# A chunked RWKV-7 and GLA layer on one core: Beta and k turned by VectorE and a DRAM bounce, the read-out without additions, and a new order

## The chip, the core and the metric

The kernel runs on one core of a Trainium2 chip. A core has five engines with instruction streams of their own, which meet only at semaphores: TensorE (PE; its weight loads are listed as PEld), VectorE (DVE), ScalarE (ACT), GpSimd (POOL) and SyncE (SP), which here issues every DMA. The metric is the device time of one execution in microseconds; lower is better.

## The reference

One inference step of one layer for a prompt of 1024 tokens and 8 single new tokens, all in float32. Two branches read the same projection of x and are merged by gates. The part around the change is the RWKV-7 branch: 16 heads of 64, taken in 8 pairs of heads.

```python
p = einsum('btd,dn->btn', x, w_in)                  # 1024 -> 9360 columns
...
prev = concatenate([shift0[:, None], p_rwkv[:, :-1]], axis=1)
pr = p_rwkv + (prev - p_rwkv) * rwkv_mu             # the token before, mixed in
r, kb, vb, g_b, w_lr, aa_lr = split(pr)
w = exp(-0.606531 * sigmoid(rwkv_w0 + tanh(w_lr) @ rwkv_w2))
a = sigmoid(rwkv_a0 + aa_lr @ rwkv_a2)
kk = normalised(kb * rwkv_k_k)
kb = kb * (1.0 + (a - 1.0) * rwkv_k_a)
# for each token and head, S is 64x64:
S = S * w + (S @ -kk) (kk * a)^T + v k^T
y = S @ r
...
m = sigmoid(gate_a) * (o_gla @ w_up_gla) + sigmoid(gate_b) * (o_rwkv @ w_up_rwkv)
y_out = layernorm(2**0.25 * x + m @ w_out)
```

The outputs are y for both groups, the last states of both branches and the last projected rows.

## The kernel before

**Tiles and stages.** The prompt is worked in two passes of 512 tokens; the 8 single tokens go with the first. Channels lie on the partitions, tokens along the free dimension. The projections are blocks of 128 output channels. Each float32 operand is split into two parts of a faster type (`xh`/`xl` and `wpart`), and a block is 8 x 3 matmuls for each of its token tiles: 256 and 264 tokens in the first pass, 512 in the second. The first pass loads the weights (`wraw`), splits them and stores the split parts to DRAM (`w`); the second reads them back. After the blocks of w_in of both passes come the two up-projections, then the output projection with the layer norm.

**A pair of heads.** `pair` runs `front`, `back`, `turn`, `chain` and `norm`. `front` makes the decays and the operands of 8 chunks of 64 tokens: `AZ` (from kk and r), `BK` (Beta, which is kk times a, and k, both divided by the decay), the masked products `GG` of the two, and the inverse of a triangular matrix for each chunk. The inverse is a loop of 31 steps on GpSimd with a multiplication and an addition in each; its operand goes to DRAM (`LD`) and comes back in another layout, and so does its result (`XD`). `back` completes the inverse on TensorE. `turn` transposes `BK` chunk by chunk on TensorE, four to a PSUM bank, with a copy back into `BK`, and then v. `chain` walks through the 8 chunks, three matmuls each (PSUM tag `pch`), and ends with the read-out: for each chunk and head three products in 64\*64 tiles, spread over the four quadrants of the array and over two PSUM banks `pY_`, one for each half of the contraction. So each output is the sum of two banks: three copies and three additions on VectorE (`places`). `norm` normalises and stores the result.

**The token shift.** `shift` evacuates a projection block: ScalarE scales it by 1 - mu (`omu`), VectorE adds mu times the same block one token earlier. In the second pass the first token needs the first pass's last one, which is kept in `tail`: one VectorE instruction on a single column, 33 times.

**The order.** All of it is written as generators of operations (`Stream`), and a planner (`Order.run`) chooses, operation after operation, which goes next, from estimated prices (`price`), the estimated time at which each engine and operand is free, and priorities (`PRIO`, `FOR_PE`, `AGE`, `ASIDE`, `URGENT`, `STAND`, `SCARCE`, `PER_ROW`). The program is the order that it finds, and each engine runs its part in that order; SP too, so a DMA that waits holds those behind it. `E` is an engine of either kind: the planner takes VectorE or GpSimd. `C` takes ScalarE or VectorE. `GATES` says how many gate blocks follow each pair's blocks, `EARLY_GATES`, `SPARE_ROWS` and `RAWS` how far gate rows and inputs are loaded ahead. `row` is a pool of 40 buffers of 128x520.

The profile attributes nearly everything to line 234, where the helper records every operation; tile names tell the groups apart. `big<-cons,wide` are the transposes of `BK` (`cons` holds the identity, `wide` is `BK`), `big<-cons,row` others, those of v among them; `big<-az,gg` and `big<-gg,wide` in 64\*64 tiles are the read-out; `row<-row,big` of 64x256 and 128x256 are its additions.

## Time and profile before

| what | us |
|---|---|
| median of three runs (1447.72 to 1448.53) | 1448.14 |
| the profiled execution, its own time | 1447.86 |
| its span, first instruction to last | 1446.1 |
| TensorE busy | 1432.1 |
| VectorE busy | 1071.7 |
| ScalarE busy | 824.3 |
| GpSimd busy | 379.6 |
| time between the profiled time and its span | 1.8 |

How to read it: busy time is the union of an engine's instructions within the span. Matmuls are pipelined: the duration of one is its latency, and neighbours overlap, so what a matmul occupies is read from the distance of starts in the timeline. A form such as "64\*64 64x64" is rows by columns of the array that the stationary operand takes, and then the size of the output. A float32 product appears as two records, a float32 transpose as one.

### The profile page before, as it was taken

The numbers are of one execution on the slowest core, as the hardware profiler recorded it, in microseconds if no ns is written. First come the engines' busy times: TensorE is split into PE (matmuls) and PEld (weight loads), VectorE is DVE, ScalarE is ACT, GpSimd is POOL, SyncE is SP. The second block draws the span as 40 slices with busy tenths as digits, with TensorE's granted clock in tenths as the row PEclk, the third lists the DMA queues.
The fourth block names the chain that finished last, engine by engine and source line by source line (L and its number), as shares of the span: only waits on it lengthen the run. The fifth ranks groups of instructions, "written<-read, shape, count | busy, mean of one in ns | idle before, by whom it ended". The sixth has DMA issues, their size and how long they took to land.

```text
span 1446.1 us, 31531 instructions
## 1 busy us (share of the span) xinstructions
PE 1432.1 (99%) x11280; PEld 1262.7 (87%) x11280; DVE 1071.7 (74%) x2213; ACT 824.3 (57%) x2035; POOL 379.6 (26%) x1138
## 2 busy tenths in 40 slices
PE   9999999999999999999999999999999999999997
PEld 8999999999999998888788888888788897897786
DVE  7687668976688767783877795978597967676585
ACT  6565658675777575754665655564556656654210
POOL 1061416142324250605060615140523050000000
PEclk9999999999999999999999999999999999999999
DMA  9786877758876688657665655646676677898842
GB/s 327 259 285 217 251 274 252 246 173 309 265 275 224 231 258 291 193 157 218 195 185 153 206 172 169 208 134 204 199 228 190 194 231 246 269 300 273 271 128 86
DMA packets 213625, 323.42 MB, mean 224 GB/s; under 512 B 91955, under 2 KB 107452, under 8 KB 213468
## 3 DMA queue, kind: packets, MB, share of 16 engines
q1 hardware_dynamic: 213468, 321.39, 69.5%
q8 instruction: 90, 1.47, 0.4%
q14 instruction: 67, 0.55, 0.1%
HBM read 201.65 MB, written 118.61 MB: 221 GB/s over the span
## 4 chain that ended last, share of the span: by engine, by line
PE 92%; DVE 4%; DMA 2%; ACT 1%; issue 1%; SPq 0%; DVEq 0%; ACTq 0%
PE proj L234 59%; PE big L234 27%; PE pch L234 6%; DVE row L234 1%; DVE wpart L234 1%; DMA wraw<-w_in 1%; DMA wraw<-w_up_gla 0%; DVE xl L234 0%; DMA row<-xT 0%; DMA row<-w_out 0%; ACT wpart L234 0%; DVE wide L234 0%; DMA row<-o_rwkv 0%; DVE XT L234 0%; ACT row L234 0%
## 5 line engine op out<-in xcount | busy, mean ns | idle before, releaser
L234 PE MATMUL proj<-xh,wpart 128*128 128x512 f32 (+3 forms) x3728 | 910.1, 328 | 0.0
L234 PEld LDWEIGHTS proj<-xh,wpart 128*128 128x128 f32 x3728 | 620.2, 188 | 51.5 <-issue 5.0
L234 PE MATMUL proj<-xl,wpart 128*128 128x512 f32 (+3 forms) x1864 | 610.0, 327 | 0.0
L234 PEld LDWEIGHTS proj<-xl,wpart 128*128 128x128 f32 x1864 | 351.3, 188 | 25.3 <-issue 2.8
L234 POOL TENSOR_TENSOR Xt<-X,wide 128x60 f32<-128x60 f32 (+24 forms) x496 | 166.1, 335 | 522.0 <-DMA wide<-LD 204.4
L234 DVE TENSOR_TENSOR row<-row 128x512 f32<-128x512 f32 (+6 forms) x348 | 180.0, 529 | 15.7 <-ACT row L234 10.5
L234 DVE TENSOR_TENSOR wpart<-wraw,wpart 128x512 fp32r<-128x512 f32 x210 | 145.8, 700 | 59.5 <-ACT wpart L234 57.0
L234 ACT CAST wpart<-wraw 128x512 fp32r<-128x512 f32 x210 | 129.7, 621 | 97.1 <-PE proj L234 50.5
L234 POOL TENSOR_TENSOR X<-X,Xt 128x60 f32<-128x60 f32 (+24 forms) x496 | 168.5, 340 | 38.7
L234 ACT ACTIVATE row<-row 128x520 f32<-128x520 f32 (+4 forms) x229 | 138.2, 610 | 14.9 <-DMA row<-sg 6.7
L234 PE MATMUL big<-xh,wpart 128*128 128x256 f32 (+3 forms) x544 | 125.7, 319 | 0.6 <-ACT xh L234 0.4
L234 DVE TENSOR_TENSOR wide<-pch,gg 64x65 f32<-64x65 f32 x224 | 49.6, 222 | 65.7 <-PE pch L234 63.6
L234 PEld LDWEIGHTS big<-xh,wpart 128*128 128x128 f32 x544 | 90.0, 188 | 8.0 <-ACT xh L234 0.6
L234 ACT COPY rh<-pch 128x130 f32<-128x130 f32 x118 | 31.7, 268 | 105.8 <-PE pch L234 104.9
L234 PE MATMUL big<-xl,wpart 128*128 128x256 f32 (+3 forms) x272 | 86.9, 320 | 0.4 <-DVE xl L234 0.3
L234 ACT COPY row<-big 128x128 f32<-128x128 f32 (+8 forms) x176 | 55.6, 341 | 54.1 <-PE big L234 50.2
L234 POOL TENSOR_TENSOR row<-row 128x256 f32<-128x256 f32 (+3 forms) x21 | 24.5, 1180 | 213.0 <-DVE row L234 122.0
L234 DVE SCALAR_TENSOR_TENSOR row<-proj,pv,row 128x255 f32<-128x255 f32 (+1 forms) x95 | 54.6, 574 | 34.5 <-ACT row L234 28.1
L234 ACT COPY wide<-pch 64x65 f32<-64x65 f32 x232 | 48.2, 208 | 52.3 <-PE pch L234 49.2
L234 ACT ACTIVATE row<-proj,omu 128x256 f32<-128x256 f32 (+1 forms) x95 | 52.0, 547 | 39.1 <-PE proj L234 37.4
L416 ACT ACT_TABLE_LOAD x56 | 71.8, 1283 | 1.0
L234 PE MATMUL big<-row 128*64 128x64 f32 (+4 forms) x648 | 64.8, 272 | 0.0
(220 smaller groups left out, 2117.5 us busy)
## 6 DMA issues: line engine op xcount, KB each, us to landing
w<-wpart SPq DMA_DIRECT2D x146, 512.0 KB
wpart<-w SPq DMA_DIRECT2D x146, 512.0 KB
wraw<-w_in SPq DMA_DIRECT2D x146, 256.0 KB
wide<-LD SPq DMA_DIRECT2D x64, 128.0 KB
wraw<-w_up_gla SPq DMA_DIRECT2D x32, 256.0 KB
row<-w_out SPq DMA_DIRECT2D x32, 256.0 KB
wraw<-w_up_rwkv SPq DMA_DIRECT2D x32, 256.0 KB
sg<-row SPq DMA_DIRECT2D x16, 260.0 KB
```

Source lines behind the costliest of these rows:

```text
L234: ways.append((eng, lambda call=call: call(out, *args, **kw), price(eng, name, out, args, ins)))
L416: self.nc.scalar.preload_act_table_set(self.table)
```

## The change

- **Beta and k.** The 8 transposes on TensorE and 2 copies in `turn` are gone. In `front`, VectorE turns `BK` in blocks of 32x32, two instructions of 128x512, each written whole to a DRAM tile `BT`. Four DMAs read `BT` back into `BK` with the blocks in their places, 32 partitions each, in runs of 32 floats. They are issued behind steps 4, 9, 14 and 19 of GpSimd's loop.
- **The read-out.** The products with the state (`s0`) stay in 64\*64 tiles, one for each chunk and head. The two products with `uf` become one over all 128 rows, in a 128\*64 tile. Both accumulate in the same bank and half, so each output is whole, and four copies of 64x256 take the place of three copies and three additions.
- **The rate factor**, te = ka * a + (1 - ka), goes from VectorE or GpSimd to ScalarE (16 times).
- **The edge column.** In the second pass ScalarE evacuates the first column by itself, with mu times the old last token as its bias. `tail` is multiplied by mu once, when all 33 blocks of the first pass have been evacuated (`edged`); the second pass's evacuations wait for that count.
- **The order.** The planner's priorities and the constants of the gate blocks, inputs and spare rows are set anew.

```diff
-RAWS = 5
+RAWS = 6
...
-SPARE_ROWS = 11
-EARLY_GATES = 13
-GATES = [[2, 1, 3, 0, 3, 2, 2, 3], [2, 1, 2, 2, 2, 3, 1, 3]]
+SPARE_ROWS = 10
+EARLY_GATES = 12
+GATES = [[1, 1, 3, 0, 3, 2, 2, 4], [1, 1, 3, 2, 1, 3, 1, 4]]
...
-AGE = 1.593
+AGE = 2.117
...
-ASIDE = 2.254
+ASIDE = 1.655
...
-FOR_PE = {"pair": 0.502, "turn": 1.611, "chain": 0.743, "norm": 0.181, "lora": 1.468, "rank": 2.14,
-          "head": 0.532, "gate": 2.004, "state": 3.339, "out": 0.822}
-STAND, SCARCE, PER_ROW = 0.037, 0.036, 0.038
-URGENT = 1.733
+FOR_PE = {"pair": 0.438, "turn": 2.001, "chain": 1.193, "norm": 0.187, "lora": 3.947, "rank": 2.131,
+          "head": 0.435, "gate": 1.614, "state": 3.803, "out": 1.518}
+STAND, SCARCE, PER_ROW = 0.037, 0.036, 0.042
+URGENT = 2.628
...
 # shift
-            yield A.activation(dst[:, t0:t0 + m], q[:, lead:lead + m], AF.Copy, scale=omu)
+            if i:
+                yield lambda: self.edged == NRC
+                yield A.activation(dst[:, :1], q[:, :1], AF.Identity, scale=omu, bias=self.tail[:, 0, j:j + 1])
+                yield A.activation(dst[:, 1:m], q[:, 1:m], AF.Copy, scale=omu)
+            else:
+                yield A.activation(dst[:, t0:t0 + m], q[:, lead:lead + m], AF.Copy, scale=omu)
...
             if i:
-                yield V.scalar_tensor_tensor(dst[:, :1], self.tail[:, 0, j:j + 1], mu, dst[:, :1], ALU.mult, ALU.add)
                 yield A.copy(self.tail[:, 0, j:j + 1], q[:, n - 1:n])
-            elif tt == last and smp is not None:
+            elif tt == last:
+                self.edged += 1
+                if self.edged == NRC:
+                    o = PV["mu"][0]
+                    yield V.tensor_mul(self.tail[:, 0], self.tail[:, 0], self.pv[:, o:o + NRC])
+            if i == 0 and tt == last and smp is not None:
                 yield V.scalar_tensor_tensor(smp, self.shT[:, j], mu, dst[:, HT:c.n], ALU.mult, ALU.add)
...
 # front
-        yield E.tensor_scalar(te, td, self.pvec("ka", p), self.oka[:, p:p + 1], ALU.mult, ALU.add)
+        yield A.activation(te, td, AF.Identity, scale=self.pvec("ka", p), bias=self.oka[:, p:p + 1])
...
+        BT = self.dr.tile([P, NCH * P], F32, name=f"BT{c.i}{p}")
+        for f in range(2):
+            y = yield from self.row(HT)
+            yield V.transpose(y, BK_[:, f * HT:(f + 1) * HT])
+            yield self.S.dma_start(BT[:, f * HT:(f + 1) * HT], y)
+            self.free(y)
+        b5 = BT.rearrange("(a i) (x b j) -> b i x a j", a=4, b=4, j=32)
         tm = yield from self.get("Xt")
         for j in range(31):
...
+            if j % 5 == 4 and j < 20:
+                b = j // 5
+                yield self.S.dma_start(BK[32 * b:32 * b + 32].rearrange("i x (a j) -> i x a j", a=4), b5[b])
...
 # turn
-        for x in range(0, NCH, 4):
-            pt = yield from self.bank("big", [P, 4, P])
-            for n in range(4):
-                yield self.tr(pt[:, n], d.BK[:, x + n])
-            yield self.C.copy(d.BK[:, x:x + 4], pt)
-            self.free(pt)
...
 # chain
-        todo = [[[] for _ in HS] for _ in HS]
-        for x in range(NCH):
-            for h, hs in enumerate(HS):
-                ks, out = HS[1 - h], (h + 2 * x // NCH) % 2
-                todo[h][out] += [(x, d.s0[hs, x, vs[h]], AZ[hs, x, 1]), (x, uf[hs, x, vs[h]], GG[hs, x, 1, h])]
-                todo[1 - h][out] += [(x, uf[ks, x, vs[h]], GG[ks, x, 1, h])]
-        yield together([self.P.matmul(pY[r][HS[o], x], w, m, start=(n == 0), stop=(n == len(todo[0][0]) - 1),
-                                      skip_group_check=True)
-                        for n in range(len(todo[0][0])) for r in range(2) for o in range(2) for x, w, m in [todo[r][o][n]]])
-        n = NCH // 2 * C
-        places = [(d.y[:, :n], slice(0, P), slice(0, n))] + [(d.y[hs, n:], ks, slice(n, 2 * n)) for hs, ks in (HS, HS[::-1])]
-        for y, ps, ns in places:
-            yield self.C.copy(y, pY_[0][ps, ns])
-        for y, ps, ns in places:
-            yield V.tensor_add(y, y, pY_[1][ps, ns])
+        H = NCH // 2
+        half = [[(x, HS[(h + x // H) % 2]) for x in range(NCH)] for h in range(2)]
+        order = [(h, x + H * f) for x in range(H) for f in range(2) for h in range(2)]
+        yield together([self.P.matmul(pY[h][half[h][x][1], x], d.s0[HS[h], x, vs[h]], AZ[HS[h], x, 1], start=(x % H == 0),
+                                      stop=False, skip_group_check=True) for h, x in order] +
+                       [self.P.matmul(pY[h][half[h][x][1], x], uf[:, x, vs[h]], GG[:, x, 1, h], start=False, stop=True,
+                                      skip_group_check=True) for h, x in order])
+        y3 = d.y.rearrange("p (c t) -> p c t", c=NCH)
+        for f in range(2):
+            xs = slice(f * H, f * H + H)
+            for h in range(2):
+                yield self.C.copy(y3[HS[h], xs], pY[h][half[h][f * H][1], xs])
```

More of the change, by code (lines that the diff above doesn't have):

```diff
@@ L84 @@
 BIAS = 0.133
-ASIDE = 2.254
-PRIO = {"evacuate": 0.333, "pair": 0.326, "turn": 0.743, "chain": 0.251, "norm": 0.15, "x": 0.413,
-        "lora": 0.709, "rank": 1.159, "head": 0.246, "gate": -0.151, "w": 0.32, "out": 0.552, "state": 0.049,
-        "block": 0.583}
-FOR_PE = {"pair": 0.502, "turn": 1.611, "chain": 0.743, "norm": 0.181, "lora": 1.468, "rank": 2.14,
-          "head": 0.532, "gate": 2.004, "state": 3.339, "out": 0.822}
-STAND, SCARCE, PER_ROW = 0.037, 0.036, 0.038
-URGENT = 1.733
+ASIDE = 1.655
+PRIO = {"evacuate": 0.333, "pair": 0.326, "turn": 0.426, "chain": 0.251, "norm": 0.026, "x": 0.745,
+        "lora": 0.67, "rank": 1.291, "head": 0.198, "gate": -0.057, "w": 0.32, "out": 0.555, "state": 0.039,
+        "block": 0.735}
+FOR_PE = {"pair": 0.438, "turn": 2.001, "chain": 1.193, "norm": 0.187, "lora": 3.947, "rank": 2.131,
+          "head": 0.435, "gate": 1.614, "state": 3.803, "out": 1.518}
+STAND, SCARCE, PER_ROW = 0.037, 0.036, 0.042
+URGENT = 2.628
 SIGMOID, EXP = "sigmoid_and_others", "natural_log_exp_and_others"
@@ L1816, in run_all @@
     def run_all(self):
+        self.edged = 0
         self.chained, self.headed, self.decayed, self.backs = -1, 0, 0, 0
```

## The prediction

> **What bounds the kernel now.** Read the engines' shares and the slices first, then the busy time in stretches, then who waited for whom.
>
> ```profile
> PE 1432.1 (99%) x11280; PEld 1262.7 (87%) x11280; DVE 1071.7 (74%) x2213; ACT 824.3 (57%) x2035; POOL 379.6 (26%) x1138
> PEclk9999999999999999999999999999999999999999
> PE 92%; DVE 4%; DMA 2%; ACT 1%; issue 1%; SPq 0%; DVEq 0%; ACTq 0%
> ```
>
> TensorE is busy for 99% of the span at the full granted clock, and the chain that ended last is 92% TensorE. VectorE has a quarter of the span free, ScalarE two fifths. The stretches (start:end, then the busy time of PE, PEld, DVE, ACT, POOL, the clock, the DMA engines' share and GB/s) say that this is no average:
>
> ```profile
> 0.00:200.00 200.00, 197.25 (x1764) 188.21 (x1765) 149.06 (x301) 122.38 (x300) 53.08 (x156) 1.00 0.81 268
> 200.00:400.00 200.00, 199.78 (x1968) 192.64 (x1968) 146.19 (x305) 135.94 (x355) 71.10 (x214) 1.00 0.76 252
> 400.00:600.00 200.00, 198.35 (x1780) 185.29 (x1779) 153.76 (x318) 132.16 (x343) 62.34 (x169) 1.00 0.75 251
> 800.00:1000.00 200.00, 200.00 (x1438) 163.83 (x1437) 162.75 (x347) 113.45 (x286) 72.79 (x214) 1.00 0.59 178
> 1300.00:1446.00 146.00, 138.44 (x638) 110.46 (x636) 95.26 (x163) 33.94 (x68) 0.00 (x0) 0.98 0.58 191
> ```
>
> Of the span's 14.0 idle us (1446.1 - 1432.1) the first 200 us hold 2.75 and the last 146 us 7.56; all between holds 3.7. The view of waits agrees; its longest row for PE is the first instruction of the program:
>
> ```profile
> PE pch L539 <- DVE warm L536: 1.1, 1, 1.1
> ```
>
> So the rule for this case is: a microsecond of TensorE work removed is nearly a microsecond of time, because projection matmuls are always ready to move up; work moved among the other engines costs nothing until one of them keeps TensorE waiting.
>
> **The change part by part.** *Beta and k (the 128 transposes).* `turn` loses 8 TensorE transposes for each of 16 pairs, 128 in all, and 32 copies out of PSUM.
>
> ```profile
> L234 PE MATMUL big<-cons,wide 128*128 128x128 f32 x128 | 19.2, 272 | 0.0
> ```
>
> The 272 ns are one transpose's latency, which overlaps its neighbours. What it occupies is the distance between starts; the timeline shows the second four of a pair, and then the four of v that stay:
>
> ```profile
> 636.10 0.60 PE L234 MATMUL big<-cons,wide 128*128 128x128 f32 x4
> 636.53 0.60 PE L234 MATMUL big<-cons,row 128*128 128x128 f32 x4
> ```
>
> Four in 0.43 us, 0.108 us each: 128 x 0.108 = 13.8 us off TensorE. Nothing is late in their place: the next instruction is the v transpose or a projection matmul.
>
> *The read-out.* A pair now has 48 products in 64\*64 tiles, four tiles at a time; afterwards 16 in 64\*64 and 16 in 128\*64, where two tiles share the array. One fp32 product makes two records. First a pair's read-out, its first and last piece and what follows, then 12 products of the other form (in the GLA heads) and what follows:
>
> ```profile
> 600.96 0.27 PE L234 MATMUL big<-az,gg 64*64 64x64 f32 x1
> 602.25 0.34 PE L234 MATMUL big<-gg,wide 64*64 64x64 f32 x9
> 602.52 0.73 PE L234 MATMUL proj<-xh,wpart 128*128 128x512 f32 x2
> 603.08 0.40 PE L234 MATMUL proj<-xl,wpart 128*128 128x512 f32 x1
> 603.32 0.40 PE L234 MATMUL proj<-xh,wpart 128*128 128x512 f32 x1
> ```
>
> ```profile
> 621.60 0.92 PE L234 MATMUL big<-row 128*64 128x64 f32 x24
> 622.45 0.50 PE L234 MATMUL big<-part,headsr 128*128 128x512 f32 x1
> ```
>
> 48 products take 602.52 - 600.96 = 1.56 us, 0.0325 each; 12 take 0.85 us, 0.071 each. New: 16 x 0.0325 + 16 x 0.071 = 0.52 + 1.13 = 1.65 us, 0.09 more for a pair, 1.5 us for 16. A third fewer products, and no less TensorE time, since a 128\*64 product takes half the array where the 64\*64 takes a quarter. Each group has a start and an end besides, and there are now two; I take +2 us. From below the bound is 0 (the two run into each other without a seam). From above: the products come in the order left, right, right, left half of the columns, which no row shows; should the halves not overlap, 16 products cost twice 1.13, and the read-out is 1.2 us longer, 19 us in all.
>
> The Trainium skill (TensorEngine Tiling (Array Packing), section Key Properties) says that a change of the tiling mode, though not of the tile, drains the TensorE. By it the seam inside the read-out is real, and the sum has the 2 us, not 0; the trace's two groups end with a longer gap than their steady pace, which agrees.
>
> *VectorE and ScalarE.* In order: the block transposes' price, two read-out additions, the k factor, the edge column; then, of ScalarE, the copies of Beta and k, an Identity with scale and bias on 512 columns, the read-out copies, and a tiny activation.
>
> ```profile
> L234 DVE STREAM_TRANSPOSE row<-row 128x512 f32<-128x512 f32 x16 | 11.3, 707 | 0.4
> L234 DVE TENSOR_TENSOR row<-row,big 64x256 f32<-64x256 f32 x32 | 13.4, 420 | 1.0
> L234 DVE TENSOR_TENSOR row<-row,big 128x256 f32<-128x256 f32 x16 | 6.7, 420 | 5.4 <-ACT row L234 5.2
> L234 DVE TENSOR_SCALAR row<-row,pv,oka 128x512 f32<-128x512 f32 x16 | 8.8, 547 | 0.6
> L234 DVE SCALAR_TENSOR_TENSOR row<-tail,pv,row 128x1 f32<-128x1 f32 x33 | 7.6, 230 | 0.0
> ```
>
> ```profile
> L234 ACT COPY wide<-big 128x512 f32<-128x512 f32 x28 | 16.4, 586 | 10.0 <-PE big L234 9.6
> L234 ACT ACTIVATE row<-row,pv 128x512 f32<-128x512 f32 x16 | 11.6, 723 | 0.0
> L234 ACT COPY row<-big 64x256 f32<-64x256 f32 x30 | 11.0, 367 | 0.7
> L234 ACT COPY row<-big 128x256 f32<-128x256 f32 x16 | 6.0, 372 | 20.6 <-PE big L234 20.6
> L234 ACT ACTIVATE row<-proj 128x8 f32<-128x8 f32 x16 | 2.9, 181 | 0.0
> ```
>
> VectorE gains 32 x 0.707 = 22.6 and loses 13.4 + 6.7 + 8.8 + 7.6 and four copies: about -16 us. ScalarE loses 16.4, gains 16 x 0.723 = 11.6, 33 small activations at 0.18 to 0.3 (6 to 10), and 64 copies of 64x256 for 16 + 30 (23.5 - 17.0 = 6.5): about +10 us, 58% of the span. Both at nothing: TensorE's work hides them, and neither is near full. Were that cover gone, the 10 us of ScalarE would be their price at most. The new wait (`edged`) holds the first evacuations of the second pass until all 33 rows of the first are out, plus one small multiply; four gate rows lie between, and they cover it.
>
> *The bounce.* Each pair adds six DMAs on SP: two writes of 256 KB in runs of 2 KB and four reads of 128 KB in runs of 128 B; together 16.8 MB and 16 x (256 + 4096) = 69,632 packets.
>
> ```profile
> DMA packets 213625, 323.42 MB, mean 224 GB/s; under 512 B 91955, under 2 KB 107452, under 8 KB 213468
> q1 hardware_dynamic: 213468, 321.39, 69.5%
> ```
>
> By bytes that is 16.8 / 321.39 x 69.5 = 3.6 points of the DMA engines' span; by packets at the mean price 69,632 / 213,468 x 69.5 = 22.7 points. That mean packet has 1.5 KB, the new ones mostly 128 B, so I take 5. The busiest stretch with pairs goes from 0.81 to about 0.86, below full. A round trip of such runs is in the trace: four writes of 32 KB to `XD`, and the first read back, which waits for them.
>
> ```profile
> 615.66 2.54 SPq L234 DMA_DIRECT2D XD<-X  x4
> 619.71 0.83 SPq L234 DMA_DIRECT2D XT<-XD  x2
> ```
>
> 4.05 us with their issue. The reads stand behind steps 4, 9, 14 and 19 of POOL's 31, each of two operations:
>
> ```profile
> L234 POOL TENSOR_TENSOR Xt<-X,wide 128x60 f32<-128x60 f32 (+24 forms) x496 | 166.1, 335 | 522.0 <-DMA wide<-LD 204.4
> L234 POOL TENSOR_TENSOR X<-X,Xt 128x60 f32<-128x60 f32 (+24 forms) x496 | 168.5, 340 | 38.7
> ```
>
> The last read has 11 steps x 0.675 = 7 us before the loop ends, and the chain that uses it comes after `back`. So the bounce is hidden. The added wait stands on SP: the write of `BT` waits for VectorE, and behind it in SP's order are the weight loads, for which TensorE waits. SP waits already, and long:
>
> ```profile
> SPq L234 <- PE proj L234: 231.4, 102, 6.1
> SPq L234 <- POOL wide L234: 12.2, 5, 9.1
> ```
>
> 9.1 us in one piece starved nobody: four buffers of 12 matmuls, at 0.24 us each in the second pass (603.08 to 603.32), cover 11 us. Cost taken: 0; price if a load comes late, some us each time.
>
> *Precedences.* The priorities order the whole program anew. Of TensorE's 14 idle us most lie at the start and the end, 3.7 between; with small gaps that the modelled ends hide a better order can win some 6 us, a worse one can lose as much or more. I take 0.
>
> Sum against the profiled execution (1447.86 us, span 1446.1 and 1.8 around it; 0.3 below the median 1448.14): -13.8 + 2 = -11.8, so **1436 us**.
>
> **The rivals.** *The order wins too*: the idle time inside goes, 6 us more, 1430 us. For it: fewer copies stand between `back` and the chain; against: there is little left to win.
>
> *The gain is given back*: removed work returns as waits, from weights late behind SP's new waits, or from more small gaps. About 1447 us. For it: everything is in a new order; against: projections fill any hole.
>
> *The column halves don't overlap*: 1448 - 14 + 19 = 1453 us. For it: their new order; against: neighbours of the group at 621.60 did overlap.
>
> *The bounce fills the DMA engines* (slower). Place: the first pass, which also stores its weights; mean share 0.773 over 600 us, so 136 us are free. Its half of the bounce costs 0.227 x 1446 / 2 = 164 us at the mean packet's price: 28 us too much, 1436 + 28 = 1464 us. It decides from 136 / 164 x 75 = 62 ns a packet on (75 = 0.695 x 16 x 1446 us / 213,468). Against it: 1024 packets of `XD` went in 4.05 us on 16 engines, at most 63 ns each, issue and latency included.
>
> The Trainium skill speaks against this change (VectorE: DVE Perf Modes, The three transpose paths): a transpose by a DMA's strides is far slower than the hardware's own, and the rules there send a 128x128 transpose to TensorE. By it the last rival is likelier than I make it; but here VectorE turns inside the blocks, and the DMA moves whole runs of 32.
>
> **How the numbers follow.** Forecast (1432 to 1440): 0.66. The order wins too: 0.12. The gain given back, 1441 to 1452: 0.12, of which a third faster by over 0.2% (2.9 us, about what a measurement of this kernel can tell from no change), a half within, the rest slower. Halves: 0.05. DMA: 0.05. Faster 0.66 + 0.12 + 0.04 = 0.82; same 0.06; slower 0.02 + 0.10 = 0.12. The range leaves out the two dear rivals and the outer ends: 1428 to 1446.
>
> **What would show it.** Right: TensorE's records fall by 128 + 512 to 10,640, with its share still 99%; no `big<-cons,wide` row; the read-out of a pair, from its first record to the next projection, 1.6 to 1.75 us; DMA share 73 to 76%; VectorE about 15 us less, ScalarE 10 more. Wrong: waits of PE on `wpart` or on the chain's tiles, a read-out of 2.5 us and more, a DMA share near 0.95 in the first 600 us, or TensorE idle over 20 us.

## The result, and the profile after

| what | before | after |
|---|---|---|
| median, us (range, runs) | 1447.86 (1446.38 to 1448.53, 5) | 1454.87 (1451.81 to 1455.76, 5) |
| the profiled execution: its time / its span | 1447.86 / 1446.1 | 1452.62 / 1450.8 |
| TensorE busy / idle within the span | 1432.1 / 14.0 | 1425.3 / 25.5 |
| ScalarE / VectorE / GpSimd busy | 824.3 / 1071.7 / 379.6 | 812.0 / 1065.5 / 385.3 |

The ratio is 1.0044, with a 95% interval of 1.003 to 1.0059: slower by some 7 us, where 12 us less were forecast. From the page of after, the engines' busy time, the DMA queue and the chain that ended last:

```profile
PE 1425.3 (98%) x10640; PEld 1251.5 (86%) x10640; DVE 1065.5 (73%) x2184; ACT 812.0 (56%) x2019; POOL 385.3 (27%) x1146
q1 hardware_dynamic: 284636, 338.18, 74.2%
PE 83%; DVE 6%; DMA 5%; ACT 3%; SPq 1%; issue 1%; DVEq 0%; ACTq 0%
```

TensorE has its 10,640 records and the DMA share is 74.2%, both as foretold. TensorE's share is 98%, not 99, and its 25.5 us of idle time are a sign of being wrong that the prediction named (over 20). The chain is only 83% TensorE (92% before): VectorE, the DMAs and ScalarE now stand in it. In the busy time by stretches (start:end, length, then PE, PEld, DVE, ACT, POOL, clock, DMA share, GB/s) the loss has its places:

```profile
0.00:200.00 200.00, 194.62 (x1705) 184.96 (x1706) 144.94 (x292) 121.89 (x302) 55.93 (x155) 1.00 0.83 278
400.00:600.00 200.00, 196.08 (x1732) 182.35 (x1732) 156.55 (x313) 126.96 (x339) 57.53 (x172) 1.00 0.80 260
800.00:1000.00 200.00, 196.95 (x1290) 159.21 (x1289) 159.59 (x329) 105.69 (x272) 57.25 (x186) 1.00 0.67 188
1000.00:1200.00 200.00, 196.65 (x1379) 165.72 (x1378) 141.67 (x299) 117.84 (x281) 67.34 (x198) 1.00 0.79 234
1300.00:1450.80 150.80, 143.32 (x682) 115.85 (x680) 98.66 (x169) 35.66 (x70) 0.00 (x0) 0.99 0.55 186
```

The first 200 us idle 5.4 us (2.75 before), 400 to 600 us 3.9 (1.65 before), 800 to 1000 us 3.1 (none before), 1000 to 1200 us 3.4 (0.4 before); the end is as it was. The row of before that the prediction doesn't show:

```profile
1000.00:1200.00 200.00, 199.56 (x1532) 171.03 (x1531) 153.08 (x317) 116.61 (x274) 63.73 (x202) 1.00 0.68 210
```

Who waited, in after (in total, how often, and the longest, in us):

```profile
PE pch L234 <- DVE wide L234: 3.0, 5, 1.0
PE pch L234 <- ACT rh L234: 3.0, 1, 3.0
PE proj L234 <- DMA wpart<-w: 2.8, 2, 1.4
ACT wpart L234 <- DMA wraw<-w_in: 20.0, 12, 4.4
ACT wpart L234 <- DMA w<-wpart: 9.1, 5, 2.8
```

Before, TensorE's longest wait was 1.1 us, at the program's start; now there is one of 3.0. And ScalarE waits 20.0 us for new weights, where before it was

```profile
ACT wpart L234 <- DMA wraw<-w_in: 4.6, 4, 2.0
```

The longest stall, in the timeline of after (start, duration, engine, operation, and in brackets the idle time before it and its releaser), shows how such a wait reaches TensorE:

```profile
176.88 1.30 SPq L234 DMA_DIRECT2D gla_s<-row  x1
181.82 0.38 SPq L234 DMA_DIRECT2D row<-state_gla  x1
...
182.81 0.38 SPq L234 DMA_DIRECT2D wraw<-w_in  x1
...
187.64 0.62 ACT L234 CAST wpart<-wraw 128x512 fp32r<-128x512 f32 x1 [4.45 <-DMA wraw<-w_in]
188.16 0.50 ACT L234 ACTIVATE row<-row 128x256 f32<-128x256 f32 x1
...
188.57 0.25 ACT L234 COPY rh<-pch 128x130 f32<-128x130 f32 x1
...
188.87 0.49 PE L234 MATMUL pch<-rh,XT 128*128 128x130 f32 x2 [3.00 <-ACT rh L234]
```

SP issues nothing between 178.18 and 181.82 us, since the load of `row` waits for a store. SP's waits in this stretch (176 to 190 us), and the same row for the whole of before:

```profile
SPq L234 <- DMA gla_s<-row: 3.6, 1, 3.6
```

```profile
SPq L234 <- DMA gla_s<-row: 1.6, 2, 1.1
```

The load of `wraw` behind it goes out at 182.81; it is the 52nd, and the split of weights that waits 4.45 us at the head of ScalarE's stream is the 52nd too. Behind it stands a copy of 0.25 us that the chain on TensorE needs and that waits for no weights. Three in-order streams pass the delay on, and nothing of the changed arithmetic is in it. In e1 below, which leaves the bounce's DMAs out, SP stands at the same place for 3.5 us (178.76 to 182.26).

By the distances of starts, TensorE's work changed by -13.8 us (transposes, as in the prediction) and +2.4 us (read-out, from the rows shown below). Take as the usual pace the median distance of starts for each pair of neighbouring forms: the gaps of over 0.1 us above it sum to 36.3 us before and 51.4 after, +15.1. The sums depend on what is called the usual pace; two other ways to take it gave differences of 16 and 17 us. The balance, +3.7, is near the span's +4.7.

### The profile page after: what moved, and what is told of

The parts are those of the page before. It is cut to its first block, busy times and chain, and to the rows that moved or that the text cites. A ratio compares the mean times of both kernels' runs of the same rounds, so it can differ in the third digit from the quotient of the medians.

```text
span 1450.8 us, 30348 instructions
## 1 busy us (share of the span) xinstructions
PE 1425.3 (98%) x10640; PEld 1251.5 (86%) x10640; DVE 1065.5 (73%) x2184; ACT 812.0 (56%) x2019; POOL 385.3 (27%) x1146
## 3 DMA queue, kind: packets, MB, share of 16 engines
q1 hardware_dynamic: 284636, 338.18, 74.2%
## 4 chain that ended last, share of the span: by engine, by line
PE 83%; DVE 6%; DMA 5%; ACT 3%; SPq 1%; issue 1%; DVEq 0%; ACTq 0%
PE proj L234 52%; PE big L234 26%; PE pch L234 6%; DVE row L234 2%; SPq L234 1%; ACT row L234 1%; DMA wraw<-w_in 1%; DVE wide L234 1%; DMA wpart<-w 1%; DVE gg L234 1%; DMA w<-wpart 1%; DVE wpart L234 1%; DMA gla_s<-row 0%; DMA row<-vd 0%; DMA shift_s<-sto 0%
## 5 line engine op out<-in xcount | busy, mean ns | idle before, releaser
L234 PEld LDWEIGHTS proj<-xh,wpart 128*128 128x128 f32 x3680 | 612.8, 188 | 57.7 <-issue 7.6
L234 DVE TENSOR_TENSOR row<-row 128x512 f32<-128x512 f32 (+8 forms) x339 | 176.4, 532 | 10.8 <-ACT row L234 5.4
L234 ACT ACTIVATE row<-row 128x512 f32<-128x512 f32 (+3 forms) x229 | 137.6, 610 | 14.3 <-DVE row L234 6.8
L234 PE MATMUL big<-xh,wpart 128*128 128x256 f32 (+3 forms) x592 | 136.3, 318 | 0.0
L234 POOL TENSOR_TENSOR row<-row 128x512 f32<-128x512 f32 (+5 forms) x30 | 27.3, 919 | 347.9 <-DVE row L234 195.4
L234 PEld LDWEIGHTS big<-xh,wpart 128*128 128x128 f32 x592 | 98.1, 189 | 7.6 <-issue 0.8
L234 ACT COPY row<-big 128x128 f32<-128x128 f32 (+6 forms) x188 | 61.0, 346 | 61.8 <-PE big L234 52.0
L234 PE MATMUL big<-xl,wpart 128*128 128x256 f32 (+3 forms) x296 | 93.6, 316 | 0.6 <-DVE xl L234 0.6
L234 PE MATMUL big<-row 128*64 128x64 f32 (+5 forms) x680 | 69.7, 287 | 0.5 <-DVE row L234 0.4
```

The costliest lines, as they stand in the source:

```text
L234: ways.append((eng, lambda call=call: call(out, *args, **kw), price(eng, name, out, args, ins)))
```

## The experiments

The question: are those 15 us a price of the edits, or of the order? An order here is a whole program, so an edit moves everything. Three kinds of run part the two. *Pinned*: an operation keeps its place and its price in the planner, but issues something else or nothing. *Redrawn*: the work stays, and a constant of the planner moves by less than 0.2%, which draws another order. *Swapped*: one kernel with the other's constants. The pinned runs rest on these:

```python
def ghost(op):          # planned as ever, issues nothing
    op.ways = [(eng, lambda: None, cost) for eng, _, cost in op.ways]
...
def also(op, *calls):   # issues calls behind op, unknown to the planner
...
def instead(op, *calls):
    op.ways = [(eng, (lambda eng=eng: [call(eng) for call in calls]), cost) for eng, _, cost in op.ways]
```

In the table, "half clock" is worked out from the busy time in stretches of 2 us: the time that TensorE spent at half of its full clock, the last 10 to 40 us of the program left out (there the clock falls as the work runs out). Idle is the profiled span less TensorE's busy time. Both are of the one profiled execution, which can lie at an end of the range: in e5, e9 and e12 it is the longest, in p6 the shortest. Beside each run stood the kernel before, with medians of 1447.7 to 1448.4 us.

| run | median us (range, runs) | ratio to before, 95% | idle | half clock |
|---|---|---|---|---|
| before | 1447.86 (1446.38 to 1448.53, 5) | | 14.0 | 0 |
| after | 1454.87 (1451.81 to 1455.76, 5) | 1.0044, 1.003 to 1.0059 | 25.5 | 0 |
| e1_ghost_bounce | 1452.01 (1448.94 to 1456.14, 10) | 1.0027, 1.0015 to 1.0039 | 21.2 | 10.2 |
| e13_ghost_all | 1453.9 (1445.25 to 1458.44, 10) | 1.0033, 1.0016 to 1.0051 | 24.1 | 6.8 |
| e2_ghost_turn | 1438.36 (1436.71 to 1439.9, 4) | 0.9928, 0.991 to 0.9946 | 17.4 | 0 |
| p7_turn_only | 1439.24 (1438.44 to 1440.03, 4) | 0.9939, 0.992 to 0.9957 | 16.9 | 0 |
| p11_long_packets | 1441.84 (1439.47 to 1444.65, 5) | 0.9955, 0.9941 to 0.9968 | 18.1 | 0 |
| p6_dma_only | 1447.24 (1444.95 to 1452.13, 10) | 1.0002, 0.999 to 1.0014 | 18.9 | 0 |
| p5_later | 1450.83 (1448.05 to 1456.61, 10) | 1.0025, 1.0013 to 1.0036 | 20.5 | 3.4 |
| p1_bounce | 1457.37 (1456.91 to 1457.91, 4) | 1.0069, 1.0054 to 1.0084 | 28.2 | 0 |
| p8_pieces | 1457.97 (1456.15 to 1459.04, 4) | 1.0068, 1.0052 to 1.0085 | 28.9 | 10.2 |
| p12_no_wait | 1467.24 (1464.91 to 1468.24, 4) | 1.0127, 1.0113 to 1.0141 | 36.7 | 20.4 |
| p4_read | 1452.68 (1451.29 to 1453.34, 5) | 1.0033, 1.002 to 1.0046 | 16.1 | 0 |
| p3_all | 1462.34 (1461.59 to 1464.31, 4) | 1.0106, 1.009 to 1.0121 | 30.0 | 6.8 |
| e5_before_order2 | 1462.7 (1461.85 to 1468.21, 4) | 1.0114, 1.0093 to 1.0135 | 26.0 | 17.1 |
| e9_before_order3 | 1463.63 (1462.86 to 1465.1, 4) | 1.0107, 1.0091 to 1.0124 | 23.8 | 13.7 |
| e4_before_newconst | 1458.85 (1458.74 to 1460.16, 4) | 1.0073, 1.0054 to 1.0092 | 22.7 | 3.4 |
| e7_after_order2 | 1458.34 (1454.13 to 1460.62, 4) | 1.0074, 1.005 to 1.0098 | 26.3 | 6.8 |
| e12_after_order4 | 1467.97 (1455.94 to 1472.47, 4) | 1.0126, 1.0079 to 1.0173 | 34.9 | 20.4 |
| e3_after_oldconst | 1464.35 (1463.96 to 1465.83, 4) | 1.011, 1.0093 to 1.0127 | 31.9 | 10.2 |

### In the new order: what does the bounce cost?

```diff
-            yield V.transpose(y, BK_[:, f * HT:(f + 1) * HT])
-            yield self.S.dma_start(BT[:, f * HT:(f + 1) * HT], y)
+            yield ghost(V.transpose(y, BK_[:, f * HT:(f + 1) * HT]))           # e13 alone
+            yield ghost(self.S.dma_start(BT[:, f * HT:(f + 1) * HT], y))       # e1, e13
...
-                yield self.S.dma_start(BK[32 * b:32 * b + 32].rearrange("i x (a j) -> i x a j", a=4), b5[b])
+                yield ghost(self.S.dma_start(BK[32 * b:32 * b + 32].rearrange("i x (a j) -> i x a j", a=4), b5[b]))
```

Both leave Beta and k unturned.

> The changed kernel with its six bounce DMAs of each pair left out, while the planner still counts them, so that every engine's order is that of the changed kernel (VectorE still turns the blocks; Beta and k reach the chain unturned). Theory B, the bounce: its packets and its place in SP's queue make weights land late, ScalarE waits for them in order and TensorE behind it: 1434 to 1441 us, and ScalarE's waits on wraw fall from 20 us to about 5. Theory O, the new order itself is worse, whatever the bounce moves: 1449 us or more. Theory E, the other edits (edge, rate factor, read-out): 1449 or more as well.

> As e1_ghost_bounce (the changed kernel in its own order without the bounce's DMAs), and VectorE's 32 block transposes left out as well; the planner counts all of them. Theory V (22.6 us of VectorE in a pair's path are not free): 1440 to 1447, against 1452 with the transposes. Theory O (the loss lies in the order that the planner found, whatever the bounce does): 1448 to 1452.

Without the 96 DMAs after's order takes 1452.0 us, without the block transposes too 1453.9: 1 to 3 us under after, with intervals that overlap its own. Theory B (1434 to 1441) and theory V (1440 to 1447) fall, and e13 is above its theory O (1448 to 1452) as well. TensorE's work is then some 11 us below before's, and the time still 4 to 6 above. ScalarE's wait for weights is there in e1, and no shorter:

```profile
ACT wpart L234 <- DMA wraw<-w_in: 22.5, 15, 3.6
```

So within this order most of the loss isn't in the bounce as executed. It lies in the order, which still holds the bounce's planned places (theory O), or in the three other edits, which both runs keep (theory E). These two runs can't part O from E; p4 and p3 below price those edits in the old order.

### In the old order: each part of the bounce

e2 drops the 128 transposes and their copies; the others add to it parts of the bounce at pinned places.

```diff
-                yield self.tr(pt[:, n], d.BK[:, x + n])
-            yield self.C.copy(d.BK[:, x:x + 4], pt)
+                yield ghost(self.tr(pt[:, n], d.BK[:, x + n]))      # e2 and all below
+            yield ghost(self.C.copy(d.BK[:, x:x + 4], pt))
...
+            turned[(0, 10)[f]] = lambda f=f: self.nc.vector.transpose(self.yb, BK_[:, half[f]])      # p5, p7
+            turned[(3, 13)[f]] = lambda f=f: self.nc.sync.dma_start(BT[:, half[f]], self.yb)         # p5; p6: from BK_ itself
+        for b, j in enumerate((18, 20, 22, 24)):                                                     # p5, p6
+            turned[j] = lambda b=b: self.nc.sync.dma_start(
+                BK[32 * b:32 * b + 32].rearrange("i x (a j) -> i x a j", a=4), b5[b])
...
-            yield self.G.tensor_add(X[:, 0:ni, j + 1:], X[:, 0:ni, j + 1:], tv)
+            yield also(self.G.tensor_add(X[:, 0:ni, j + 1:], X[:, 0:ni, j + 1:], tv), *([turned[j]] if j in turned else []))
```

p5 computes everything. e2 turns nothing; p7 leaves out the DMAs and p6 VectorE's transposes, so Beta and k aren't turned there either.

> The kernel before, in its own order, with the 128 TensorE transposes of Beta and k and their 32 copies left out and nothing in their place (Beta and k reach the chain unturned). If TensorE work removed is time, as the prediction had it: 1448 - 13.8 = 1434 us, 1432 to 1437. If the freed TensorE time turns into waits for something that TensorE had hidden: over 1440.

> As p5_later, without its DMAs: VectorE turns the blocks into a buffer that nobody reads. Theory V: 1446 to 1451. Theory B: 1439 to 1442. If both p6_dma_only and p7_turn_only lie half way, the two costs add up.

> As p5_later, without VectorE's transposes: the two writes take BK itself and the four reads bring it back (so Beta and k reach the chain with their blocks moved and not turned inside), the same DMAs at the same places. Between 1438.4 (e2_ghost_turn, nothing in the place of the transposes) and 1450.8 (p5_later): theory V 1439 to 1442, theory B 1446 to 1451.

> As p1_bounce (the order of the kernel before, Beta and k turned by VectorE and DRAM, everything computed), with VectorE's two transposes and the DMAs moved out of the way: the first transpose stands behind step 0 of GpSimd's loop, the second behind step 10, the four reads behind steps 18 to 24. Theory V (p1_bounce lost its gain because 1.4 us of VectorE stood ahead of the head sums for which TensorE waits): 1439 to 1447. Theory B (it is the DMAs, wherever they stand): 1453 to 1458, as in p1_bounce. Theory F (the chosen order has no room: anything that shifts a pair's chain comes out at TensorE): between the two, 1447 to 1455.

By the medians: the removed work is worth 9.6 us, between the two ranges expected of e2 (in its profile TensorE's busy time falls by 11.5, and idle time grows by 3.4). VectorE's 22.6 us of added work cost 0.9, which the intervals of p7 and e2 don't tell from nothing. The DMAs alone cost 8.9, as theory B had it. Both together cost 12.5, more than the gain; p5 lies in the range of theory F. The prediction had 0 for all of it. Among SP's waits in p6 is this row:

```profile
SPq L1301 <- DMA BT<-wide: 16.9, 8, 5.0
```

Two runs ask whether that is SP standing before reads that wait for their writes, or the DMA engines' time for short runs. In p11 the four reads keep places and waits, and take rows of 4 KB. p12 moves as many bytes in runs as short, meant to wait for nothing. Neither turns anything.

```diff
# p11, against p6
-                BK[32 * b:32 * b + 32].rearrange("i x (a j) -> i x a j", a=4), b5[b])
+                BK_[32 * b:32 * b + 32, :NCH * P], BT[32 * b:32 * b + 32])
# p12, against p6
+        b5 = self.bt0.rearrange("(g i) (r q j) -> g q i r j", g=2, q=2, j=32)      # bt0: zeros, written once
...
-            turned[(3, 13)[f]] = lambda f=f: self.nc.sync.dma_start(BT[:, half[f]], BK_[:, half[f]])
+            turned[(3, 13)[f]] = lambda f=f: self.nc.sync.dma_start(BT[:, half[f]], self.zb)
...
-                BK[32 * b:32 * b + 32].rearrange("i x (a j) -> i x a j", a=4), b5[b])
+                self.zb[64 * (b // 2):64 * (b // 2) + 64].rearrange("i (r j) -> i r j", j=32), b5[b // 2, b % 2])
```

> Before's order with the bounce's DMAs alone, as in p6_dma_only, at the same places of SP's queue and with the same waits; only the runs are other: each of the four reads takes 32 rows of 4 KB from BT to BK where p6 takes 1024 runs of 128 bytes. VectorE's block transposes and TensorE's transposes are left out, so Beta and k are not turned. p6 stood at 1447.2 us, some 9 above the ghosted transposes without DMAs (e2_ghost_turn 1438.4). Theory A, packets: the 9 us are the time of the 131,072 short packets on the 16 DMA engines, which every weight load shares; then this run falls to 1439 to 1441. Theory B, queue: the 9 us are SP standing before the writes (which wait for BK) and the reads (which wait for the writes), with the weight loads behind it; then the long packets change little, 1445 to 1448.

> As p6_dma_only, with as many DMAs of the same bytes and run lengths at the same places of SP's queue, but moving a buffer of zeros that nothing else uses: the writes no longer wait for BK, and the reads come from a DRAM tile that was written once, into that buffer, so nothing waits for them. Beta and k are not turned. Theory A, packets: the traffic is unchanged, so 1446 to 1448 as p6. Theory B, queue: SP no longer stands, so 1438 to 1441. If both this run and p11 stay near 1447, it is neither alone, and the second or third place in which the order is disturbed matters more than the cause; if both fall, the two work together: a wait that is long because the packets are slow.

SP's wait before the reads is no shorter in p11:

```profile
SPq L1301 <- DMA BT<-wide: 18.3, 9, 5.1
```

and yet the time falls from 1447.2 to 1441.8, near the 1439 to 1441 that the theory of the packets gave. So some 5.4 of the 8.9 us belong to the short runs: the ratios' intervals of p6 and p11 lie apart. 3.5 are left for SP's waits and the traffic itself; there the intervals of p11 and e2 still touch. The short runs are half of the 131,072 that the expectation counts. The other half is in before as well, by the count of packets in before, p6 and p11:

```profile
DMA packets 213625, 323.42 MB, mean 224 GB/s; under 512 B 91955, under 2 KB 107452, under 8 KB 213468
DMA packets 284792, 340.18 MB, mean 236 GB/s; under 512 B 159027, under 2 KB 174524, under 8 KB 284636
DMA packets 221305, 340.18 MB, mean 236 GB/s; under 512 B 93492, under 2 KB 108989, under 8 KB 221149
```

p12 missed both expectations, by a fault of its own: all reads go into one buffer, so each waits for the one before it. Of its SP:

```profile
SPq L1305 <- DMA zb<-BT: 92.6, 32, 5.6
SPq L1305 <- DMA BT<-zb: 16.7, 9, 4.3
```

It didn't take SP's waits away but raised them from 16.9 to 109.3 us, and was 20.0 us slower than p6 with nobody waiting for the data. So it doesn't settle what p6's 16.9 us of standing cost; it shows that 109.3 us of it are dear.

The place matters as much. p1 issues the block transposes as soon as `BK` is there (on VectorE ahead of `kb`), with the reads at the change's own steps; p8 cuts the write in four.

```diff
# p1
-            yield E.tensor_mul(BK[hs, :, C - h * C:2 * C - h * C], bc(kb)[hs], tb3[hs, :, 1:])
+            turned = [lambda f=f: self.nc.vector.transpose(ys[f], BK_[:, f * HT:(f + 1) * HT]) for f in range(2 * h)]
+            yield also(E.tensor_mul(BK[hs, :, C - h * C:2 * C - h * C], bc(kb)[hs], tb3[hs, :, 1:]), *turned)
...
# p8, against p5 (the two transposes and two writes go)
+            turned[(0, 5, 9, 13)[f]] = lambda part=part, yb=yb: self.nc.vector.transpose(yb, BK_[:, part])
+            turned[(3, 7, 11, 15)[f]] = lambda part=part, yb=yb: self.nc.sync.dma_start(BT[:, part], yb)
```

> The kernel before in its own order, with Beta and k turned as in the change: the planner still counts the 8 transposes and 2 copies of a pair, but they are not issued; VectorE's two block transposes, the two writes and the four reads are issued behind neighbouring operations, without the planner's knowledge (one half passes through the buffer of L, the other through a buffer of its own). Everything is computed. Theory L (a new order is what costs, the parts of the change are sound): 1438 to 1443, the 1438.4 of the run that only left the transposes out, and up to 5 for VectorE's 22.6 us and the DMAs. Theory B (the bounce starves TensorE): 1448 or more.

> As p5_later, everything computed, with VectorE's transposes in four pieces of 128x256 behind steps 0, 5, 9 and 13 of GpSimd's loop. Theory V, if what counts is how long VectorE is held in one piece (0.7 us before, about 0.43 now): 1443 to 1448, below the kernel before. If its total counts: 1450 to 1453, as four pieces take 0.3 us more than two.

Both compute everything, and both lose 19 to 20 us against e2. p1 lies in the range of theory B (1448 or more), not in that of theory L, by which the parts of the change were sound; p8 is above both of its ranges. In p1 the block transposes stand ahead of the head sums' operands; TensorE's longest row of waits is

```profile
PE big L234 <- ACT part L234: 7.7, 9, 1.4
```

which p5, with the transposes some steps later, doesn't have. In p8 the buffers come free later, so SP and VectorE wait oftener for the writes (15.3 us of VectorE, 11 times, against 7.6 us, 4 times, in p5).

### The read-out alone, and all four edits

```diff
# p4: the new matmuls and copies in the places of the old ones, the additions not issued
+        yield instead(op, *[lambda e, h=h, x=x: mm(pY[h][half[h][x][1], x], d.s0[HS[h], x, vs[h]], AZ[HS[h], x, 1],
...
-            yield V.tensor_add(y, y, pY_[1][ps, ns])
+            yield ghost(V.tensor_add(y, y, pY_[1][ps, ns]))
```

p3 is p1 with p4's read-out, the rate factor on ScalarE in its old place, and the split edge column. Both compute everything.

> The kernel before in its own order with the new read-out alone (64*64 and 128*64 tiles, four copies in the places of three, the three additions not issued). TensorE pays 2.4 us for the seam, VectorE is freed of 20 us. Theory F: near 1450, 1448 to 1453, as the read-out stands at the end of a pair's chain and nobody waits for it soon. If the read-out is a cause of the loss: over 1455.

> All four edits of the change in the order of the kernel before: the bounce as in p1_bounce, the read-out in the new tiles with its four copies in the places of the old three and the additions gone, the rate factor and the edge column on ScalarE in the places of the VectorE instructions. Everything is computed. Theory L: 1438 to 1446, with 2.4 for the seam in the read-out. If an edit itself costs what the changed kernel lost: 1452 or more, and the distance to p1_bounce says that it is not the bounce.

Timeline of after, one pair's new read-out:

```profile
618.08 0.70 PE L234 MATMUL big<-az,gg 64*64 64x64 f32 x32
618.70 1.15 PE L234 MATMUL big<-gg,wide 128*64 128x64 f32 x32
619.79 0.50 PE L234 MATMUL proj<-xh,wpart 128*128 128x512 f32 x1
```

1.71 us against 1.56 before, 0.15 more for a pair and 2.4 for 16; the halves of the columns do overlap. Yet p4 is 5.0 us slower than before, as theory F had it. In this order the saved additions buy nothing back, and 2.6 us come on top. p3, the whole change in before's order, is 14.5 us slower than before. That is over 1452, the reading that an edit itself costs what the changed kernel lost. It is p1's 9.5 and p4's 5.0, so the rate factor and the edge column add nothing that can be seen.

With p5 in p1's place, an estimate for the edits in before's order is -9.6 + 12.5 + 5.0 = +7.9 us. So the edits turn the forecast's 12 us into a loss of 8 to 14.5 us without any new order, though at places that were not planned for them. The changed kernel, in its own order, loses 7.0.

### Other orders of the same work

```diff
-TABLE = 1.28
+TABLE = 1.281        # e5 (before), e7 (after); e9 (before): 1.279
...
-LANDED = 0.648
+LANDED = 0.649       # e12 (after)
```

e3 is after with all of before's constants, e4 before with all of after's. All six compute everything.

> The changed kernel with all planner constants of the kernel before. Theory O: the new constants are what costs, so 1434 to 1441 us. Theory B: the bounce is still there, 1447 to 1456. Theory L, any order that was not chosen by measuring costs several us over the chosen one: over 1450.

> The kernel before with the planner constants of the changed kernel. Theory B: 1446 to 1450 us, the constants are innocent. Theory O: 1455 to 1465. Theory L: several us over 1448.

> The kernel before with one planner constant moved by less than a thousandth (the price of an activation table load, 1.281 for 1.28 us), which gives another order of the same work. Theory L: 1452 to 1460, as a new order costs several us over one that was chosen. If orders don't matter much: 1446 to 1450.

> The changed kernel with the same small move of the same constant. Theory L in its strong form (the changed kernel's own order is one like any other): within 1450 to 1462, on either side of 1454.9. If its order was chosen well and the loss lies in the work: 1455 to 1460, never below.

> The kernel before with the price of a table load at 1.279 instead of 1.28 us: a third order of the same work. Theory L (the order of the kernel before is one chosen among many, and its neighbours are slower): 1455 to 1465. If e5_before_order2 was a single bad draw: 1447 to 1452.

> The changed kernel with the planner's allowance for a landed DMA at 0.649 instead of 0.648 us: another order of its work. Theory L: 1452 to 1462, and on the mean of its orders below that of the orders of the kernel before, since TensorE has 11 us less to do. If the changed kernel loses for a reason that every order shares and the kernel before doesn't have: the mean of its orders is above.

Before's work in three other orders: 1458.9, 1462.7, 1463.6, mean 1461.7. After's: 1458.3, 1464.4, 1468.0, mean 1463.6. So the kernel before holds an order 11 to 16 us better than its neighbours; after's own, 1454.9, is 3 to 13 better than its neighbours. e5 (1462.7) and e12 (1468.0) are slower than even theory L had them. e4 fits theories O and L alike. e3 refutes theory O: with the old constants the changed kernel isn't near 1434 to 1441 but 9.5 us slower than with the new.

With orders drawn alike, the two programs can't be told apart by three draws each: the means differ by 1.8 us, with a standard error of some 3 us as the medians scatter. The 12 us of the forecast would have shown. Two things follow. A new order of the same work costs as much as the change was to win, and in these orders, too, the edits show no gain.

Nor is ScalarE's wait for weights what makes an order slow in general. In e7 and e12, orders near after's, it is 17.4 and 27.6 us; but in e5 and e9, 15 to 16 us slower than before, it is no longer than before's 4.6:

```profile
ACT wpart L234 <- DMA wraw<-w_in: 3.9, 2, 3.7
```

```profile
ACT wpart L234 <- DMA wraw<-w_in: 3.3, 3, 1.7
```

There TensorE waits for VectorE and ScalarE; e5's longest, in its timeline:

```profile
1112.00 0.50 PE L234 MATMUL big<-part,headsr 128*128 128x512 f32 x1 [2.27 <-DVE part L234]
```

Part of that spread is the clock. The same stretches of e5 and of before, the columns as above (the clock is the third number from the end):

```profile
1108.00:1112.00 4.00, 1.73 (x9) 1.11 (x8) 2.97 (x6) 3.94 (x6) 0.00 (x0) 1.00 0.57 129
1112.00:1116.00 4.00, 2.22 (x23) 1.28 (x23) 2.66 (x7) 3.96 (x8) 0.00 (x0) 0.82 0.16 52
1116.00:1120.00 4.00, 4.00 (x23) 3.48 (x16) 3.94 (x6) 2.02 (x6) 0.00 (x0) 0.50 0.00 0
1120.00:1124.00 4.00, 4.00 (x19) 3.50 (x18) 3.29 (x7) 3.95 (x10) 0.00 (x0) 0.83 0.17 66
```

```profile
1108.00:1112.00 4.00, 4.00 (x18) 3.22 (x18) 3.87 (x9) 3.97 (x8) 0.00 (x0) 1.00 0.78 175
1112.00:1116.00 4.00, 4.00 (x30) 2.48 (x29) 3.10 (x6) 2.28 (x6) 0.00 (x0) 1.00 0.96 330
```

In e5 TensorE is busy for 3.95 of 8 us; at their end the clock is halved, for some 7 us, in most of which TensorE looks fully busy. e5's profile has 17.1 us at half clock, which lose 8.5 us if TensorE had work throughout; that is two fifths of the 20.3 us by which its span exceeds before's.

## Why the prediction was wrong

**TensorE's work: right.** 10,640 records, no transposes of `BK`, and e2 won 9.6 of the 13.8 us; the rest came back as idle time. The read-out's +2 measured +2.4 as work, within the bounds. The seam that the Trainium skill gave (TensorEngine Tiling (Array Packing), Key Properties) is in the trace of after: between the two groups lie 0.15 us, where the longest distances within them are 0.04 to 0.05 us once each has started. Alone in the old order (p4) the read-out cost 5.0, of which the sum had no term for the 2.6 of waits.

**VectorE and ScalarE at nothing: right for VectorE's transposes,** at 0.9 us (p7), if they stand late enough; at p1's place TensorE waited for the head sums' operands. The sizes were off, and no run shows that this cost time: VectorE fell by 6 us and not 16, ScalarE fell by 12 instead of rising by 10. Of that, 7.6 us are activation tables (50 loads for 56; e5 and e9 have 58), and some 10 us are copies and splits that the planner gave to VectorE instead of ScalarE. The edge column's small activations cost 0.35 us each, not 0.18 to 0.3.

**The bounce, "Cost taken: 0": a step that failed.** In the old order its DMAs cost 8.9 us, some 5.4 of them for the reads in short runs, and with VectorE's turn 12.5. The term failed because it asked whether the data is there when the chain needs it, and whether the mean share stays below 1. Both held: no wait of after names `wide<-BT`, and the share is 74.2%. But every weight load shares the DMA engines and SP's order with it. The sentence "9.1 us in one piece starved nobody" took the deepest wait of an order that fits its waits, and not the state of the buffers at the places of the new ones. That weights came late is argued for p6 and not shown: ScalarE waits 9.6 us for them against e2's 6.9, and TensorE's longest waits there are on ScalarE's `Xt` and on the input `xT`. The rival with full DMA engines (1464) is out: by an estimate from the two queue rows (74.2% of 16 x 1450.8 us, less 69.5% of 16 x 1446.1) the 71,168 more packets took 16 ns each, against its 62. The slow DMA transpose that the Trainium skill names (VectorE: DVE Perf Modes, The three transpose paths) agrees with these 8.9 us only in sign, as the price here falls on other work. In the new order e1 puts the DMAs at some 3 us, with an interval that reaches 0.

**"Precedences ... I take 0": the other step that failed,** and with both the rule under them, that projections are always ready to move up and work on the other engines costs nothing. Projections are ready when their weights are, and these pass SP's, ScalarE's and VectorE's in-order streams; the same streams hold the operands of the head sums and the chain. TensorE's gaps grew by some 15 us where the sum had 0. The 99% of before was a property of one order, not of the work: moving one constant by 0.08% cost 15 to 16 us (e5, e9). "Some 6 us" either way was too small; these runs put +11 to +16 on a new order of before's work. Nothing in the trace of before showed that a second order could be as good, and nothing there gave this size either. The rival "the gain is given back" (1447) named the mechanism in part, weights late and more gaps, and was too small by 8 us. The rival of the column halves (1453) came near the time by luck, not by its mechanism: they overlap.

**How the miss divides between the two steps stays open.** From the forecast to the median it is 19 us. In before's order the edits alone are enough for it (+7.9 to +14.5 where -12 was forecast). In after's own order the bounce as executed is only 1 to 3 of it (e1, e13), and the rest lies with the order and the other edits. No run holds after's order without the read-out or with before's work, so the shares can't be added up.

**The sum, redone,** on the profiled pair: -13.8 + 2.4 of work and +15.1 of waits make +3.7, and the span grew by 4.7. The medians are 7.0 apart. After's five executions have mean granted clocks of 0.996 to 0.999, on average 0.9974; before's 62 beside the runs average 0.9987. By an estimate that is 0.0013 x 1453 = 1.9 us, most of the remaining 2.3; but the fastest of the five, 1451.81 us, has 0.997, so the clock isn't all of the scatter.

What also stays open: which of the new constants puts the loads late in SP's order; how much of p6's remaining 3.5 us is SP's waiting; how wide the spread of orders really is, with three redrawn ones on each side. Of the kernels that compute everything none beat the kernel before; the nearest is p5, by +0.25%.

## What to carry to other kernels

Where a program is one planned order at 99% of its bounding engine, less work on that engine isn't worth its time until the new order is as good, and until what replaces the work costs the other streams nothing: price a new order as a term of its own, and measure the spread by moving an unrelated constant a little. To learn what an edit itself costs, pin the order and leave out or add only that edit. Before a round trip through DRAM is called hidden, ask which loads share its queue and engines, and what stands behind them on the engine that consumes them.

## What the runs showed of the hardware

A stall of TensorE can cost more than its length. In the 20 profiles the time at half clock, summed in stretches of 2 us and away from the end, is 0, 3.4, 6.8, 10.2, 13.7, 17.1 or 20.4 us: whole multiples of 3.4, each of which loses up to 1.7. Whether a stall trips it depends on more than the stall. After and e1 share one order and stall near the same place; after (first) keeps its clock, e1 (second) loses it:

```profile
186.00:188.00 2.00, 0.00 (x0) 0.00 (x0) 0.00 (x0) 0.36 (x1) 0.00 (x0) 1.00 0.90 347
188.00:190.00 2.00, 1.13 (x9) 1.13 (x10) 1.71 (x4) 2.00 (x7) 0.00 (x0) 1.00 1.04 418
190.00:192.00 2.00, 2.00 (x18) 2.00 (x17) 1.99 (x4) 1.41 (x4) 0.00 (x0) 1.00 1.03 414
```

```profile
188.00:190.00 2.00, 0.03 (x1) 0.03 (x1) 0.61 (x2) 1.26 (x4) 0.00 (x0) 1.00 1.03 415
190.00:192.00 2.00, 2.00 (x13) 2.00 (x14) 1.99 (x6) 1.97 (x6) 0.00 (x0) 0.73 1.03 413
192.00:194.00 2.00, 2.00 (x11) 2.00 (x11) 1.99 (x4) 0.63 (x2) 0.00 (x0) 0.50 1.04 412
```

The Trainium skill (TensorE: Matmul & The Clock Gate, Part 1: The HAM clock gate) describes this: activity is judged in free-running windows of about 3.4 us, and an idle window halves the clock until a busy one. The multiples of 3.4 and the chance in it agree. One thing differs: in e1 and e5 no such window was idle throughout. TensorE's longest idle time before the loss of clock is 2.01 us here in e1 and 2.27 us in the stretch of e5 above, while after keeps its clock through 3.00 us; so a window that is busy in part can be enough. It fits that e13, with a stall of 4.2 us, scatters by 13 us in ten executions, while the kernel before, whose longest wait is 1.1 us, stayed within 1445.8 to 1451.5 in 62. After's own five, 4 us apart, are too few to show it.
